# First block's two attentions: probabilities become the stationary operand of the value product, values are streamed, and the division by the softmax sum comes after it

## The chip, the cores and the metric

One core of one Trainium2 chip runs the whole program. The metric is the device time of one execution in microseconds (us), the median of several runs. The core has a matrix engine (TensorE, PE in the profile, its weight loads PEld), a vector engine (DVE), a scalar engine (ACT), a small general engine (POOL) and DMA queues that SyncE (SP) issues. Each engine works through its own queue in order and waits on semaphores of the others.

## What is computed

Two networks follow each other on 512 tokens of width 1024. The change touches only the first one, `first_block`, which has two layers. In each layer one wide projection feeds three branches: a banded attention, a convolution and a dense causal attention. Their outputs are gated, summed and followed by an MLP. The two attentions, cut to what matters:

```python
def swa_attention(q, k, v, sinks, bias, mask):        # 8 query heads, 2 key/value groups, width 64
    scores = einsum('bnqhgd,bnkhd->bnqkhg', qb, kk) * 64 ** -0.5 + bias     # a block of 128 queries,
    scores = where(mask, scores, NEG_INF)                                    # 256 keys: own and last block
    m = maximum(scores.max(axis=3, keepdims=True), sink)
    p = exp(scores - m)
    p = p / (p.sum(axis=3, keepdims=True) + exp(sink - m))
    out = einsum('bnqkhg,bnkhd->bnqhgd', p, vv)

def attend_block(args):                               # mla: 8 heads, blocks of 128 queries, values 64 wide
    sc = (einsum('bqhd,bkhd->bhqk', qn, k_nope) + einsum('bqhd,bkd->bhqk', qp, k_pe)) * scale
    sc = where(key_idx[None, :] <= q_idx[:, None], sc, NEG_INF)
    p = softmax(sc, axis=-1)
    return einsum('bhqk,bkhd->bqhd', p, v)
```

## The kernel before

Activations are kept channel-major: a tile has 128 channels on the partitions and the 512 tokens on the free axis. A projection (`gemm`, `mm3`, L230 to L232) splits each fp32 operand into a high and a low part and adds three products into one PSUM tile `ps_g`, for each of eight chunks of 128 input channels. These products of 128x512 are most of the program. The weights stream in by DMA (`raw`), ACT makes the high part (`whi`, L223) and DVE the low part (`wlo`, L224).

`mix_first` weaves generators: `mla` runs against `inputs` (projections), in layer 0 also against `prep_bias`, and `swa` runs against `branch(2, ...)` (projections again). `weave` fixes the order in which the steps are recorded. The framework then orders each engine's queue by its own plan, so that projection products stand between the steps of an attention. PSUM is split by tag: three banks `g`, two `sc` (scores), and one each of `m`, `tr` (transposes) and `y` (attention output).

`mla` goes over four pairs of heads (`hp`). For each head and each block of 128 queries (`qb`, which sees (qb+1)*128 keys): scores on PE (L740), causal mask, maximum and scaling on DVE, exponential with the row sum on ACT (L771), reciprocal on DVE (L773), a second ACT pass that multiplies the probabilities by it (L774), transposes on PE (L745), and one ACT copy for each 128x128 block into `pT` (L747). After all four query blocks four products follow (L750): the stationary operand is `vt` (128 keys x 64 values), the probabilities stream through (up to 512 queries), and the result lands channel-major in 64 of the 128 rows of `ps_y`, which is then split in high and low part (L203, L204).

`swa` goes over four blocks of queries. For each group `g` of four heads: scores (L796, contraction over 64 rows of `q` and `kk`, the rows of that group), bias added on DVE (L798) into `S`, maximum, exponential (L812), reciprocal, the ACT pass that divides (L818), transposes (L822), a copy to `pT` (L824), and a product with 64 values as stationary operand and 512 columns of probabilities (L825). At the end of a query block `yhi` and `ylo` are cut from `ps_y` (L830, L831).

In PE rows the profile shows an fp32 product as two MATMUL rows with a weight load each, an fp32r product (the projections) or a transpose as one.

Of the kernel before, what the change touches and what calls it, by code (L numbers as in the profile page):

```python
# [20 lines left out]
P = 128  # L21
# [6 lines left out]
class Build:  # L28
# [652 lines left out]
    def mla(self, l, cq, ckv, kpe, out):  # L681
# [28 lines left out]
        for hp in range(4):  # L710
            if hp % 2 == 0:
                ps = self.gemm(W("w_qup", 4 + hp // 2), qs)
                x = self.ch("x", tag="tmp")
                nc.scalar.copy(out=x, in_=ps)
                sw = self.shuffle16(x)
                nc.vector.tensor_tensor(out=x, in0=x, in1=self.cosT, op=ALU.mult)
                nc.vector.tensor_tensor(out=sw, in0=sw, in1=self.sinT, op=ALU.mult)
                qp = self.ch("qp")
                nc.vector.tensor_tensor(out=qp, in0=x, in1=sw, op=ALU.add)
            qh = [self.ch("qh", tag="qh") for _ in range(2)]  # L720
            kh = [self.ch("kh", tag="qh") for _ in range(2)]
# [12 lines left out]
            for i in range(2):  # L734
                h = 2 * hp + i
                pT = [self.ch("pT", tag="pT") for _ in range(4)]
                for qb in range(4):
                    n = (qb + 1) * P
                    ps = self.psum("sc")
                    nc.tensor.matmul(ps[:, :n], qh[i][0:96, qb * P:n], kh[i][0:96, 0:n], start=True, stop=True)  # L740
# [12 lines left out]
            out.append(self.split(yps, tag="y2"))  # L753
# [7 lines left out]
    def softmax_causal(self, ps, n, scale):  # L761

# [11 lines left out]
        nc.scalar.activation(out=pr, in_=pr, func=AF.Copy, scale=r)  # L774
        self.pr = pr

    def swa(self, l, q, kk, v, out):
# [4 lines left out]
        for b in range(4):  # L782
# [3 lines left out]
            yps = self.psum("y")  # L786
            for g in range(2):
                rows = slice(64 * g, 64 * g + 64)
                bias = self.tl([P, 4, 256], F32, "bias")
                nc.sync.dma_start(out=bias, in_=self.biasD[b, 4 * g:4 * g + 4].rearrange("h q k -> q h k"))  # L790
                S = self.tl([P, 4, 256], F32, "S")
                for pr in range(2):
                    ps = self.psum("sc")
                    for i in range(2):
                        c = 2 * pr + i
                        nc.tensor.matmul(ps[:, i * N:(i + 1) * N], q[c][rows, b * P:(b + 1) * P],  # L796
                                         kk[rows, k0:k0 + N], start=True, stop=True)
                    nc.vector.tensor_tensor(out=S[:, 2 * pr:2 * pr + 2, :N],  # L798
                                            in0=ps[:, :2 * N].rearrange("p (i n) -> p i n", i=2),
                                            in1=bias[:, 2 * pr:2 * pr + 2, 256 - N:], op=ALU.add)  # L800
# [3 lines left out]
                sk = sink[:, 4 * g:4 * g + 4]  # L804
                nc.vector.tensor_tensor(out=m, in0=m, in1=sk, op=ALU.max)
                nc.vector.tensor_scalar(out=nm, in0=m, scalar1=-1.0, scalar2=None, op0=ALU.mult)
                es = self.sm("es", 4, "sw4")
                nc.vector.tensor_tensor(out=es, in0=sk, in1=m, op=ALU.subtract)
# [8 lines left out]
                for c in range(4):  # L817
                    nc.scalar.activation(out=S[:, c, :N], in_=S[:, c, :N], func=AF.Copy, scale=r[:, c:c + 1])  # L818
                for kb in range(nk):
# [5 lines left out]
                    nc.tensor.matmul(yps[rows], v[:, b - nk + 1 + kb, rows], pT, start=kb == 0, stop=kb == nk - 1)  # L825
                if g == 0:
                    yield
            sl = slice(b * P, (b + 1) * P)
            for c in range(4):
                nc.scalar.copy(out=yhi[c][:, sl], in_=yps[:, c * P:(c + 1) * P])  # L830
                nc.vector.tensor_tensor(out=ylo[c][:, sl], in0=yps[:, c * P:(c + 1) * P],  # L831
                                        in1=yhi[c][:, sl].bitcast(F32), op=ALU.subtract)
            self.dump_ps(f"ya{l}_{b}", yps)
# [1678 lines left out]
```

## Time and profile before

| | |
|---|---|
| three runs | 3928.62, 3931.33, 3933.89 us; median 3931.33 |
| profiled execution | 3927.74 us, span 3925.7 us (2.0 us lie around the span) |
| PE busy, of the span | 3777.0 us (96%) |
| PEld, DVE, ACT busy | 76%, 61%, 44% |
| mean granted TensorE clock | 0.969 of full speed |
| dense attention, layers 0 and 1 | about 65 to 252 us and 960 to 1085 us of the span |
| banded attention, layers 0 and 1 | about 252 to 330 us and 1085 to 1200 us |

The profile is one execution seen from inside. Busy time says how long an engine had something in flight; idle time before an instruction is put down to what released it. The granted clock has two levels, 1.2 and 2.4 GHz, so 0.5 or 1 in a short stretch and a mean in a longer one.

### The profile page before, as it was taken

The page shows a single profiled execution, that of the slowest core. Times are in us where ns is not written, and L with a number is a line of the kernel's source. Part 1 is how long each engine was busy: PE and PEld are TensorE (multiplying, and loading weights), DVE is VectorE, ACT ScalarE, POOL GpSimd, SP SyncE. Part 2 cuts the span into 40 slices and gives each one's busy share as a digit, 9 for nine tenths or more (in the row PEclk, how much of TensorE's full clock was granted, in tenths as well). Part 3 has the DMA queues.
Part 4 walks back from the last instruction along what each step waited for, and adds up shares of the span by engine and source line. Part 5 has one row for each costly group of instructions (what it writes and reads, how often), then busy time and mean ns, then how long its engine had stood idle before and what let it go on. Part 6 is the DMA issues. An engine that isn't in the chain of part 4 may idle for free.

```text
span 3925.7 us, 54880 instructions
## 1 busy us (share of the span) xinstructions
PE 3777.0 (96%) x21506; PEld 2970.5 (76%) x21506; DVE 2397.6 (61%) x4178; ACT 1741.0 (44%) x3923; POOL 85.0 (2%) x180
## 2 busy tenths in 40 slices
PE   8999999999999999999998999999999999889998
PEld 5566888886667888778885666688888887678887
DVE  7587567665786565657646566454444574756444
ACT  4655343334653333335537788432222264533332
POOL 0000000000000000000001000000000000000000
PEclk9999999999999999999998899899999999889999
DMA  3132345442132355531110000211111212012232
GB/s 129 49 92 83 101 155 180 157 143 65 56 94 85 121 166 171 187 116 45 45 43 2 2 2 2 76 56 64 65 65 65 83 50 68 6 59 95 97 97 75
DMA packets 115699, 324.98 MB, mean 83 GB/s; under 512 B 12528, under 2 KB 34032, under 8 KB 115440
## 3 DMA queue, kind: packets, MB, share of 16 engines
q1 hardware_dynamic: 115440, 321.47, 25.4%
q8 instruction: 169, 2.77, 0.3%
q14 instruction: 90, 0.74, 0.1%
HBM read 307.27 MB, written 12.58 MB: 81 GB/s over the span
## 4 chain that ended last, share of the span: by engine, by line
PE 79%; issue 11%; ACT 5%; DVE 4%; POOL 1%; DMA 0%; POOLq 0%; DVEq 0%; SPq 0%; ACTq 0%
PE ps_g L230 20%; PE ps_g L232 20%; PE ps_g L231 20%; PE ps_mm L1564 1%; PE ps_y L750 1%; ACT B L1621 1%; PE ps_sc L740 1%; PE ps_z L1531 1%; POOL r L308 1%; PE ps_y L825 1%; PE ps_sc L796 1%; PE ps_y L1236 1%; PE ps_lv L1611 1%; PE ps_sc L454 1%; PE ps_lv L1608 1%
## 5 line engine op out<-in xcount | busy, mean ns | idle before, releaser
L230 PE MATMUL ps_g<-hi,whi 128*128 128x512 f32 (+1 forms) x4464 | 1670.5, 374 | 21.2 <-ACT whi L223 13.7
L232 PE MATMUL ps_g<-hi,wlo 128*128 128x512 f32 (+1 forms) x4464 | 1654.9, 371 | 10.5 <-DVE wlo L224 10.4
L231 PE MATMUL ps_g<-lo,whi 128*128 128x512 f32 (+1 forms) x3744 | 1401.4, 374 | 2.3 <-DVE lo L954 1.8
L223 ACT CAST whi<-raw 128x1024 fp32r<-128x1024 f32 (+3 forms) x497 | 481.7, 970 | 1241.8 <-PE ps_g L231 1064.1
L230 PEld LDWEIGHTS ps_g<-hi,whi 128*128 128x128 f32 x4464 | 847.8, 190 | 190.2 <-ACT whi L223 23.8
L232 PEld LDWEIGHTS ps_g<-hi,wlo 128*128 128x128 f32 x4464 | 847.4, 190 | 166.4 <-DVE wlo L224 17.1
L231 PEld LDWEIGHTS ps_g<-lo,whi 128*128 128x128 f32 x3744 | 709.8, 190 | 135.0 <-issue 10.5
L224 DVE TENSOR_TENSOR wlo<-raw,whi 128x1024 fp32r<-128x1024 f32 (+3 forms) x497 | 557.2, 1122 | 165.7 <-ACT whi L223 160.0
L231 PE MATMUL ps_g<-x,whi 128*128 128x512 f32 (+1 forms) x720 | 253.1, 352 | 0.0
L1130 DVE SCALAR_TENSOR_TENSOR x<-ps_g,mod,x 128x512 f32<-128x512 f32 (+1 forms) x192 | 127.0, 662 | 200.3 <-PE ps_g L232 200.1
L879 DVE SCALAR_TENSOR_TENSOR macc<-mraw,cs,macc 128x1024 f32<-128x1024 f32 x140 | 175.7, 1279 | 6.8 <-DMA mraw<-in_mod_w 6.5
L638 DVE SCALAR_TENSOR_TENSOR cv<-u,taps,cv 128x512 f32<-128x512 f32 x240 | 177.1, 744 | 1.1
L1109 DVE TENSOR_SCALAR r<-ps_g 128x512 f32<-128x512 f32 x96 | 57.6, 602 | 180.3 <-PE ps_g L232 180.2
L231 PEld LDWEIGHTS ps_g<-x,whi 128*128 128x128 f32 x720 | 138.5, 192 | 16.5 <-issue 1.6
L589 DVE TENSOR_TENSOR x<-ps_g,x 128x512 f32<-128x512 f32 x64 | 44.2, 690 | 137.8 <-PE ps_g L232 137.8
L473 DVE TENSOR_TENSOR o<-ps_g,R 128x512 f32<-128x512 f32 x76 | 52.2, 689 | 114.6 <-PE ps_g L232 111.7
L1110 ACT ACTIVATE r<-r 128x512 f32<-128x512 f32 x96 | 53.4, 557 | 145.3 <-DVE r L1109 145.3
L308 POOL TENSOR_TENSOR r<-v,mhalf 128x4 f32<-128x4 f32 (+2 forms) x30 | 38.5, 1284 | 2792.5 <-DVE v L327 2135.6
L582 DVE SCALAR_TENSOR_TENSOR r<-ps_g,R 128x512 f32<-128x512 f32 x64 | 44.0, 688 | 80.9 <-PE ps_g L232 77.0
L204 DVE TENSOR_TENSOR lo<-r,hi 128x512 fp32r<-128x512 f32 x96 | 57.6, 600 | 40.7 <-ACT hi L203 40.7
L1621 ACT COPY B<-ps_lv 32x64 f32<-32x64 f32 x384 | 77.5, 202 | 6.4
L291 ACT ACTIVATE sq<-x 128x512 f32<-128x512 f32 (+1 forms) x91 | 49.1, 543 | 70.1 <-DVE x L1130 34.7
(508 smaller groups left out, 4574.3 us busy)
## 6 DMA issues: line engine op xcount, KB each, us to landing
raw<-in_l_mlp_w SPq DMA_DIRECT2D x128, 512.0 KB, 3.5
mraw<-in_mod_w SPq DMA_DIRECT2D x96, 512.0 KB, 4.5
raw<-in_w_in SPq DMA_DIRECT2D x82, 512.0 KB, 3.4
raw<-in_w_up SPq DMA_DIRECT2D x64, 512.0 KB, 3.5
raw<-in_w_down SPq DMA_DIRECT2D x64, 512.0 KB, 3.5
raw<-in_l_w_in SPq DMA_DIRECT2D x50, 512.0 KB, 3.5
raw<-in_w_branch SPq DMA_DIRECT2D x48, 256.0 KB, 2.8
bias<-biasD SPq DMA_DIRECT2D x16, 512.0 KB, 3.9
```

The lines of the kernel that those rows point to most:

```text
L204: nc.vector.tensor_tensor(out=lo, in0=src, in1=hi.bitcast(F32), op=ALU.subtract)
L223: nc.scalar.copy(out=hi, in_=raw)
L224: nc.vector.tensor_tensor(out=lo, in0=raw, in1=hi.bitcast(F32), op=ALU.subtract)
L230: t.matmul(ps, w[0], x[0], start=start, stop=False)
L231: t.matmul(ps, w[0], x[1], start=False, stop=False)
L232: t.matmul(ps, w[1], x[0], start=False, stop=stop)
L308: self.nc.gpsimd.tensor_tensor(out=r, in0=v, in1=self.mhalf[:, :v.shape[1]], op=ALU.pow)
L638: nc.vector.scalar_tensor_tensor(out=y, in0=u[:, j:j + T], scalar=taps[:, c * 31 + j:c * 31 + j + 1], in1=y, op0=ALU.mult, op1=ALU.add)
L879: nc.vector.scalar_tensor_tensor(out=acc[s], in0=rw, scalar=self.cs[:, k, s:s + 1], in1=acc[s], op0=ALU.mult, op1=ALU.add)
L1109: nc.vector.tensor_scalar(out=t, in0=ps[s][:, :n], scalar1=0.0, scalar2=None, op0=ALU.max)
L1130: nc.vector.scalar_tensor_tensor(out=xx[c], in0=ps[:, :n], scalar=md[:, s, 5, c:c + 1], in1=xx[c], op0=ALU.mult, op1=ALU.add)
L1621: nc.scalar.copy(out=B[rows, :, j, :], in_=blocks(ps[rows, 0:64]))
```

## The change

In `mla` the loop over the two heads moves inside the loop over query blocks. The exponentials are transposed as they are, one ACT copy brings all (qb+1) blocks of them to `pT`, and qb+1 products have a 128x128 block of `pT` as stationary operand and 64 columns of `vt` as the streamed one. The result is token-major, 128 queries x 64 values, in the single bank `m`; ACT scales it by the reciprocal on the way to `yq` (L754), and when both heads have written their 64 columns PE transposes `yq` into `ps_y` (L756). The second ACT pass over the probabilities is gone.

In `swa` the outer loop goes over two halves `pr` instead of the groups: each has two heads of group 0 and two of group 1. The four score products alternate between the groups, into two `sc` banks. The bias comes in two DMAs of half the size. The ACT pass over the probabilities is gone; 128x128 blocks of `pT` are stationary and 64 values stream (L835); one DVE multiplication by the reciprocals makes `yq` (L841), and two transposes (L844) bring it to `ps_m`, from which `yhi` and `ylo` are cut.

```diff
@@ mla
-            for i in range(2):
-                h = 2 * hp + i
-                pT = [self.ch("pT", tag="pT") for _ in range(4)]
-                for qb in range(4):
-                    n = (qb + 1) * P
+            for qb in range(4):
+                n = (qb + 1) * P
+                blk = slice(qb * P, n)
+                yq = self.ch("yq", n=P, tag="tmp")
+                for i in range(2):
+                    h = 2 * hp + i
                     ps = self.psum("sc")
...
-                    self.softmax_causal(ps, n, rq[:, qb:qb + 1])
-                    pr = self.pr
+                    pr, r = self.softmax_causal(ps, n, rq[:, qb:qb + 1])
                     tp = self.psum("tr")
                     for kb in range(qb + 1):
                         nc.tensor.transpose(tp[:, kb * P:(kb + 1) * P], pr[:, kb * P:(kb + 1) * P], self.ident)
+                    pT = self.ch("pT", tag="pT")
+                    nc.scalar.copy(out=pT[:, :n], in_=tp[:, :n])
+                    cols = slice(64 * i, 64 * i + 64)
+                    ym = self.psum("m")
                     for kb in range(qb + 1):
-                        nc.scalar.copy(out=pT[kb][:, qb * P:n], in_=tp[:, kb * P:(kb + 1) * P])
+                        nc.tensor.matmul(ym[:, :64], pT[:, kb * P:(kb + 1) * P], vt[kb][:, h * 64:(h + 1) * 64],
+                                         start=kb == 0, stop=kb == qb)
+                    nc.scalar.activation(out=yq[:, cols], in_=ym[:, :64], func=AF.Copy, scale=r)
                     yield
-                for kb in range(4):
-                    nc.tensor.matmul(yps[64 * i:64 * i + 64, kb * P:], vt[kb][:, h * 64:(h + 1) * 64],
-                                     pT[kb][:, kb * P:], start=kb == 0, stop=kb == 3)
+                nc.tensor.transpose(yps[:, blk], yq, self.ident)
@@ softmax_causal
-        nc.scalar.activation(out=pr, in_=pr, func=AF.Copy, scale=r)
-        self.pr = pr
+        return pr, r
@@ swa
-            for g in range(2):
-                rows = slice(64 * g, 64 * g + 64)
+            for pr in range(2):
...
+                ps = [self.psum("sc") for _ in range(2)]
+                for i in range(2):
+                    for g in range(2):
+                        rows = slice(64 * g, 64 * g + 64)
+                        nc.tensor.matmul(ps[g][:, i * N:(i + 1) * N], q[2 * pr + i][rows, b * P:(b + 1) * P],
                                          kk[rows, k0:k0 + N], start=True, stop=True)
...
-                for c in range(4):
-                    nc.scalar.activation(out=S[:, c, :N], in_=S[:, c, :N], func=AF.Copy, scale=r[:, c:c + 1])
...
-                    nc.tensor.matmul(yps[rows], v[:, b - nk + 1 + kb, rows], pT, start=kb == 0, stop=kb == nk - 1)
+                    for c in range(4):
+                        g, h = c // 2, 2 * pr + c % 2
+                        nc.tensor.matmul(yps[:, h * P + 64 * g:h * P + 64 * g + 64], pT[:, c * P:(c + 1) * P],
+                                         v[:, b - nk + 1 + kb, 64 * g:64 * g + 64],
+                                         start=kb == 0 and c == 0, stop=kb == nk - 1, skip_group_check=True)
+                nc.vector.tensor_tensor(out=hv(yq), in0=hv(yps[:, 2 * pr * P:(2 * pr + 2) * P]),
+                                        in1=gi(r).unsqueeze(3).to_broadcast([P, 2, 2, 64]), op=ALU.mult)
+                for i in range(2):
+                    nc.tensor.transpose(yT[:, (2 * pr + i) * P:(2 * pr + i + 1) * P], yq[:, i * P:(i + 1) * P],
+                                        self.ident)
```

The order on the engines is planned anew. PE in the dense attention of layer 1, end of the first head of a pair, before (`ps_g` are projections, `pr` probabilities, operands stand as streamed, stationary):

```order
L745 MATMUL ps_tr_7635<-ident,pr_7628 128x128 x4
L232 MATMUL ps_g_7694<-hi_7059,wlo_7690 128x512
L230 MATMUL ps_g_7694<-hi_7102,whi_7689 128x512
L750 MATMUL ps_y_7490<-pT_7491,vt_7369 64x512
L750 MATMUL ps_y_7490<-pT_7492,vt_7370 64x384
L750 MATMUL ps_y_7490<-pT_7493,vt_7371 64x256
L750 MATMUL ps_y_7490<-pT_7494,vt_7372 64x128
L745 MATMUL ps_tr_7666<-ident,pr_7659 128x128
```

The same engine and layer now, last query block of the first head of a pair:

```order
L746 MATMUL ps_tr_7868<-ident,pr_7862 128x128 x4
L232 MATMUL ps_g_7975<-hi_6968,wlo_7971 128x512
L230 MATMUL ps_g_7975<-hi_7009,whi_7970 128x512
L231 MATMUL ps_g_7975<-lo_7010,whi_7970 128x512
L752 MATMUL ps_m_7875<-vt_7487,pT_7873 128x64
L752 MATMUL ps_m_7875<-vt_7488,pT_7873 128x64
L752 MATMUL ps_m_7875<-vt_7489,pT_7873 128x64
L752 MATMUL ps_m_7875<-vt_7490,pT_7873 128x64
L232 MATMUL ps_g_7975<-hi_7009,wlo_7971 128x512
L230 MATMUL ps_g_7975<-hi_7052,whi_7970 128x512
```

A value product now follows every set of transposes, 64 times in all instead of 16, with a few projection products between the transposes and it. ACT at the same place now (`ps_m` is the bank that each of these products needs):

```order
L748 COPY pT_7873<-ps_tr_7868 128x512
L727 COPY qh_7913<-qp_7571 32x512
L732 COPY kh_7914<-k_1652_7483 32x512
L754 ACTIVATE yq_7856<-ps_m_7875,rec_7866 128x64
L777 ACTIVATE pr_7886,sum_7887<-ps_sc_7881,m_7884,rq_7435 128x512
L732 COPY kh_7915<-k_1652_7483 32x512
```

The scaling that empties `ps_m` stands in ACT's queue behind two copies for the next pair of heads. PE at one set of scores of the banded attention, layer 0, before:

```order
L796 MATMUL ps_sc_2492<-o_2163,q_1587 128x256
L796 MATMUL ps_sc_2492<-o_2163,q_1705 128x256
L796 MATMUL ps_sc_2496<-o_2163,q_1825 128x256
L796 MATMUL ps_sc_2496<-o_2163,q_2000 128x256
L230 MATMUL ps_g_2546<-hi_107,whi_2541 128x512
```

And now, first where the four stand together, then where transposes stand between them:

```order
L804 MATMUL ps_sc_2871<-o_2220,q_1876 128x256
L804 MATMUL ps_sc_2872<-o_2220,q_1876 128x256
L804 MATMUL ps_sc_2871<-o_2220,q_2052 128x256
L804 MATMUL ps_sc_2872<-o_2220,q_2052 128x256
L230 MATMUL ps_g_2939<-hi_107,whi_2934 128x512
```

```order
L804 MATMUL ps_sc_2662<-o_2220,q_1876 128x256
L830 MATMUL ps_tr_2591<-ident,S_2566 128x128
L804 MATMUL ps_sc_2663<-o_2220,q_1876 128x256
L830 MATMUL ps_tr_2591<-ident,S_2566 128x128
L804 MATMUL ps_sc_2662<-o_2220,q_2052 128x256
L830 MATMUL ps_tr_2591<-ident,S_2566 128x128
L804 MATMUL ps_sc_2663<-o_2220,q_2052 128x256
```

The 16 sets were 16 unbroken runs on PE; now they are 28 runs. The 64 value products of `mla` stood in 30 runs and the 28 of `swa` in 28; their successors are products of the full array. From the projections behind the banded attention of layer 1 on, the order on PE, DVE and ACT is what it was.

## Rows read from the trace of the kernel before

**Rows 1.** The page, busy time, share of the span and instructions of TensorE.

```profile
PE 3777.0 (96%) x21506; PEld 2970.5 (76%) x21506; DVE 2397.6 (61%) x4178; ACT 1741.0 (44%) x3923; POOL 85.0 (2%) x180
```

**Rows 2.** Stretch, length, PE, PEld, DVE, ACT, POOL busy (count), clock, DMA, GB/s.

```profile
65.00:252.00 187.00, 183.33 (x798) 102.74 (x796) 122.80 (x265) 112.11 (x266) 0.00 (x0) 0.98 0.20 58
252.00:330.00 78.00, 77.60 (x326) 52.31 (x324) 69.19 (x132) 41.92 (x114) 0.00 (x0) 1.00 0.33 101
960.00:1085.00 125.00, 118.91 (x487) 79.29 (x486) 93.66 (x215) 76.70 (x203) 0.00 (x0) 0.96 0.18 59
```

**Rows 3.** Timeline of PE at L825: start, time in flight, instruction, count.

```profile
263.82 0.40 PE L231 MATMUL ps_g<-lo,whi 128*128 128x512 f32 x1
264.15 1.07 PE L825 MATMUL ps_y<-pT,tok 128*64 128x512 f32 x2
265.15 0.50 PE L232 MATMUL ps_g<-hi,wlo 128*128 128x512 f32 x1
265.49 0.40 PE L230 MATMUL ps_g<-hi,whi 128*128 128x512 f32 x1
265.73 0.40 PE L231 MATMUL ps_g<-lo,whi 128*128 128x512 f32 x1
```

**Rows 4.** Timeline of PE at a broken run of L750.

```profile
250.27 0.50 PE L230 MATMUL ps_g<-hi,whi 128*128 128x512 f32 x1
250.71 0.43 PE L750 MATMUL ps_y<-pT,vt 128*64 128x128 f32 x2
251.07 0.50 PE L231 MATMUL ps_g<-lo,whi 128*128 128x512 f32 x1
251.41 0.39 PE L232 MATMUL ps_g<-hi,wlo 128*128 128x512 f32 x1
```

**Rows 5.** Chain of waits, both attentions: start, time on the chain, instructions.

```profile
141.30 2.30 PE ps_y L750 x8
253.18 1.09 PE ps_sc L796 x8
268.43 1.92 PE ps_sc L796 x8
```

**Rows 6.** Timeline of PE at fp32 products of 128x128 stationary, 64 streamed columns.

```profile
2027.94 1.45 PE L1291 MATMUL ps_mm<-cv,t 128*128 128x64 f32 x12
2029.19 0.48 PE L230 MATMUL ps_g<-hi,whi 128*128 128x512 f32 x1
2029.51 0.40 PE L231 MATMUL ps_g<-x,whi 128*128 128x512 f32 x1
```

**Rows 7.** Timeline of PE at single transposes between projection products.

```profile
1097.60 0.48 PE L231 MATMUL ps_g<-lo,whi 128*128 128x512 f32 x1
1097.92 0.27 PE L822 MATMUL ps_tr<-ident,S 128*128 128x128 f32 x1
1097.95 0.48 PE L232 MATMUL ps_g<-hi,wlo 128*128 128x512 f32 x1
```

**Rows 8.** Timeline of PE: 64-row products of both halves of the rows.

```profile
3424.49 1.71 PE L2159 MATMUL ps_g<-qd,kd 64*128 64x128 f32 x16
```

**Rows 9.** Timeline of PE, layer 1, from one pair of heads to the next.

```profile
1006.33 0.66 PE L745 MATMUL ps_tr<-ident,pr 128*128 128x128 f32 x4 [1.50 <-ACT pr L774]
1007.85 3.88 PE L750 MATMUL ps_y<-pT,vt 128*64 128x512 f32 x8 [0.87 <-ACT pT L747]
1013.05 0.92 PE L740 MATMUL ps_sc<-kh,qh 96*128 96x128 f32 x4 [1.31 <-ACT kh L732]
```

**Rows 10.** Busy time by stretch: around the rows before.

```profile
1003.00:1022.00 19.00, 14.65 (x44) 8.97 (x43) 9.80 (x26) 12.84 (x31) 0.00 (x0) 0.73 0.29 96
```

**Rows 11.** ACT: L774 by line (min/median/max ns), two copies by form (busy, mean).

```profile
L774 ACT ACTIVATE pr<-pr,rec x64: 393/557/752, 73.1 to 1079.2; 128x128 f32<-128x128 f32 x16, 128x256 f32<-128x256 f32 x16, 128x384 f32<-128x384 f32 x16, 128x512 f32<-128x512 f32 x16
L824 ACT COPY pT<-ps_tr 128x512 f32<-128x512 f32 x28 | 16.4, 587 | 27.8 <-PE ps_tr L822 27.5
L1679 ACT COPY zs<-ps_z 128x64 f32<-128x64 f32 x96 | 20.0, 210 | 20.3 <-PE ps_z L1676 18.5
```

More of the change, by code (lines that the diff above doesn't have):

```diff
@@ L733, in mla @@
             yps = self.psum("y")
-            for i in range(2):
-                h = 2 * hp + i
-                pT = [self.ch("pT", tag="pT") for _ in range(4)]
-                for qb in range(4):
-                    n = (qb + 1) * P
+            for qb in range(4):
[4 more added lines that the diff above has]
+                    h = 2 * hp + i
                     ps = self.psum("sc")
-                    nc.tensor.matmul(ps[:, :n], qh[i][0:96, qb * P:n], kh[i][0:96, 0:n], start=True, stop=True)
-                    self.softmax_causal(ps, n, rq[:, qb:qb + 1])
-                    pr = self.pr
+                    nc.tensor.matmul(ps[:, :n], qh[i][0:96, blk], kh[i][0:96, 0:n], start=True, stop=True)
+                    pr, r = self.softmax_causal(ps, n, rq[:, qb:qb + 1])
                     tp = self.psum("tr")
@@ L785, in swa @@
             k0 = 0 if b == 0 else (b - 1) * P
-            yps = self.psum("y")
-            for g in range(2):
-                rows = slice(64 * g, 64 * g + 64)
+            yps, yT = self.psum("y"), self.psum("m")
+            for pr in range(2):
                 bias = self.tl([P, 4, 256], F32, "bias")
-                nc.sync.dma_start(out=bias, in_=self.biasD[b, 4 * g:4 * g + 4].rearrange("h q k -> q h k"))
+                for g in range(2):
+                    h = 4 * g + 2 * pr
+                    nc.sync.dma_start(out=bias[:, 2 * g:2 * g + 2],
+                                      in_=self.biasD[b, h:h + 2].rearrange("h q k -> q h k"))
                 S = self.tl([P, 4, 256], F32, "S")
[L792 to L796, printed above, removed]
+                ps = [self.psum("sc") for _ in range(2)]
+                for i in range(2):
+                    for g in range(2):
+                        rows = slice(64 * g, 64 * g + 64)
+                        nc.tensor.matmul(ps[g][:, i * N:(i + 1) * N], q[2 * pr + i][rows, b * P:(b + 1) * P],
                                          kk[rows, k0:k0 + N], start=True, stop=True)
-                    nc.vector.tensor_tensor(out=S[:, 2 * pr:2 * pr + 2, :N],
-                                            in0=ps[:, :2 * N].rearrange("p (i n) -> p i n", i=2),
-                                            in1=bias[:, 2 * pr:2 * pr + 2, 256 - N:], op=ALU.add)
+                for g in range(2):
+                    nc.vector.tensor_tensor(out=S[:, 2 * g:2 * g + 2, :N],
+                                            in0=ps[g][:, :2 * N].rearrange("p (i n) -> p i n", i=2),
+                                            in1=bias[:, 2 * g:2 * g + 2, 256 - N:], op=ALU.add)
                 m = self.sm("m", 4, "sw4")
@@ L803, in swa @@
                 nm = self.sm("nm", 4, "sw4")
-                sk = sink[:, 4 * g:4 * g + 4]
-                nc.vector.tensor_tensor(out=m, in0=m, in1=sk, op=ALU.max)
+                gi = lambda t: t.rearrange("p (g i) -> p g i", i=2)
+                sk = sink.rearrange("p (g h) -> p g h", g=2)[:, :, 2 * pr:2 * pr + 2]
+                nc.vector.tensor_tensor(out=gi(m), in0=gi(m), in1=sk, op=ALU.max)
                 nc.vector.tensor_scalar(out=nm, in0=m, scalar1=-1.0, scalar2=None, op0=ALU.mult)
                 es = self.sm("es", 4, "sw4")
-                nc.vector.tensor_tensor(out=es, in0=sk, in1=m, op=ALU.subtract)
+                nc.vector.tensor_tensor(out=gi(es), in0=sk, in1=gi(m), op=ALU.subtract)
                 nc.scalar.activation(out=es, in_=es, func=AF.Exp)
@@ L824, in swa @@
                     nc.scalar.copy(out=pT, in_=tp)
[L825 to L826 removed]
+                    for c in range(4):
[3 more added lines that the diff above has]
+                                         start=kb == 0 and c == 0, stop=kb == nk - 1, skip_group_check=True)
+                yq = self.ch("yq", n=256, tag="tmp")
+                hv = lambda t: t.rearrange("p (i g f) -> p g i f", g=2, f=64)
+                nc.vector.tensor_tensor(out=hv(yq), in0=hv(yps[:, 2 * pr * P:(2 * pr + 2) * P]),
[3 more added lines that the diff above has]
+                                        self.ident)
+                if pr == 0:
                     yield
@@ L829, in swa @@
             for c in range(4):
-                nc.scalar.copy(out=yhi[c][:, sl], in_=yps[:, c * P:(c + 1) * P])
-                nc.vector.tensor_tensor(out=ylo[c][:, sl], in0=yps[:, c * P:(c + 1) * P],
+                nc.scalar.copy(out=yhi[c][:, sl], in_=yT[:, c * P:(c + 1) * P])
+                nc.vector.tensor_tensor(out=ylo[c][:, sl], in0=yT[:, c * P:(c + 1) * P],
                                         in1=yhi[c][:, sl].bitcast(F32), op=ALU.subtract)
-            self.dump_ps(f"ya{l}_{b}", yps)
+            self.dump_ps(f"ya{l}_{b}", yT)
             yield
```

## The prediction, on record before the run

> **What bounds the kernel now.** I read busy time first: PE has something in flight for 96% of the span [rows 1]. Then the stretches with the attentions. The dense attentions last 187 and 125 us, with PE busy for 183.3 and 118.9, so PE idles 3.7 and 6.1 us there; in layer 0's banded attention it idles 0.4 of 78 us [rows 2]. PE is the bound in all of them, and projection products fill whatever time the attention leaves. So the change is worth what PE's own queue gets shorter, plus what PE's few waits lose or gain. Third, the timeline of PE, for starts from one instruction to the next: the time in flight of a row overlaps its neighbours, only starts tell what an instruction costs the queue. A projection product takes 0.23 to 0.24 us that way (265.49 to 265.73, [rows 3]).
>
> **Value products of the banded attention.** One product of 512 columns with 64 values as stationary operand stands between projections that start at 263.82 and 265.49 [rows 3]. That is 1.67 us, less two spacings of 0.23: 1.21 us. About 0.1 us of it lies ahead of its start (0.33 instead of 0.23) and 0.11 behind (265.15 to 265.49, again instead of 0.23): PE pauses when it goes from a product that uses all 128 columns of the array to one that uses 64, and back. 28 of them are 33.9 us. They are replaced by 112 products with a 128x128 stationary block and 64 streamed columns, two passes each. The trace has the same form elsewhere: twelve passes start at 2027.94, and the second projection behind them at 2029.51 [rows 6]; 1.57 less 0.23 is 1.34, or 0.112 a pass. 224 passes are 25.1 us. Gain 8.8 us.
>
> **Value products of the dense attention.** An unbroken set for one head takes 2.30 us on the chain [rows 5], with the 0.1 ahead and 0.1 behind 2.5; 16 heads are 40 us. They stand in 30 runs, so 14 sets are broken once more. What a break costs, a short run shows: projections at 250.27 and 251.41 with two passes of 128 columns between [rows 4], 1.14 less 0.46 is 0.68, of which two passes of 128 columns explain 0.2 (2560 column passes in 2.30 us). So 0.45 for a run by itself, 6 us for 14. Together 46 us, against 160 products or 320 passes of 0.112, 35.8 us. Gain 10 us.
>
> A rule of the Trainium skill speaks against both of these. "TensorEngine Tiling (Array Packing)", section Performance Considerations, recommends for 64 wide right-hand sides to swap stationary and streamed operand and to pack two column tiles, which is the form that is given up here; packed, the old 2.30 us would be 1.15 for a head, 18 us for all, and the change would cost some 17 us on this term. The trace does not bear it out: the eight passes of a head all use one half of the columns and follow each other over 2.30 us, so nothing was packed that could be lost.
>
> **Transposes added.** 32 in each attention. One between two projections costs 1097.95 less 1097.60 less 0.23, 0.12 us [rows 7]. 64 are 7.7 us. Loss.
>
> **Scores of the banded attention.** Eight passes of 256 columns are 1.92 us on the chain, of 128 columns 1.09 [rows 5]. The difference says 0.83 us for eight times 128 columns; what is left of the 1.09, 0.26, and the 0.2 around a run as above make 0.47 us for each run. The 16 sets were 16 runs and are 28 in the new order: 12 more runs, 5.6 us lost. Against that the two groups use different halves of the array's rows, and alternate. Do such products run side by side? L2159 has eight passes of 128 columns on one half and then eight on the other. Its sixteen are in flight for 1.71 us [rows 8]; one after the other they would need 0.26 and 1.66, and 0.27 until the last one lands (the flight of a transpose, [rows 7]), 2.2. Half a us is gained at the seam alone, so I take overlap as real. Of the 16 sets six alternate without a break, five in part and five not at all (pairs of one group, or single products between transposes). A full one saves 0.83 us, 0.42 in the first query block; in all 6 to 7 us. Scores thus cost 0 with overlap, 5.6 us without.
>
> **Sum on PE's queue**: 8.8 + 10 - 7.7 - 0 = 11 us less; without overlap 5.5.
>
> **Waits.** ACT loses 64 passes of 0.557 us (median of L774, [rows 11]), 36 us in the dense attention, and 64 more passes in the banded one. It gains 64 scalings of 128x64, 0.21 each by the nearest row [rows 11], 13 us. That matters where PE waits for ACT, above all at the change of head pairs in layer 1: waits of 1.50 for L774, 0.87 for L747 and 1.31 for L732 [rows 9], and behind them TensorE is granted 0.73 of its clock over 19 us [rows 10], at which 5.1 us are lost. I count half of these 3.7 and 5.1 us as won, 4.4 us: the pass of 0.73 us at this place goes, the copies and casts stay. Against it stand new hops. A value product now follows each of 64 sets of transposes instead of 16. From the start of the last transpose it takes 0.27 us until it lands [rows 7] and 0.59 for the longest copy [rows 11], 0.86; the order puts three projections (0.69) and the transpose's own 0.12 there, 0.81. So 0.05 us short where nothing else is in ACT's queue, 3 us in all. The bounds: nothing, if shorter copies leave slack, and 10 us, if one hop in four meets a copy of 0.59 us ahead of it on ACT. Net 1 us won; bounds 9 us won, 10 lost.
>
> **Counted at nothing.** The 16 multiplications of `yq` on DVE: at most 0.59 us each (an ACT copy of twice the columns), 4.7 us in a layer, beside 69.2 busy of 78 [rows 2]; they fit, barely, and convolution steps move later. Without that cover they cost up to 4.7 us a layer. The 16 more DMA issues for the bias move the same bytes; the next `S` needs them only after the transposes of the last one, and PE idles 0.4 us in that stretch, so there is slack now; a late bias would stall one set of scores.
>
> All of it against the profiled execution, 3927.7 us: 12 us less is 3915.7. The median of the runs shown is 3.6 us higher, and so is the forecast: 3931.3 - 12 = 3919 us.
>
> **The rivals.** (1) *Nothing measurable.* The scores do not overlap, or the many short runs eat it, which leaves 5.5 us; and the new hops cost what the lighter ACT gives. 3926 us, between 3924 and 3939, as its bounds on the hops fall. For it: the 28 runs, and how little cover 0.81 us against 0.86 is. Against it: rows 8.
> (2) *All waits at the change of pairs vanish*, with them the lost clock: 11 and 9 us, 3911 us. For it: the three waits of layer 1 hang on one queue, ACT, which gets lighter just there. Against it: two of them are for copies that stay.
> (3) *Slower: one bank for every hop.* `ps_m` is one bank. Each of the 64 value products must wait until ACT's scaling L754 has emptied it for the one before, and that scaling stands in ACT's queue behind copies (two of about 0.59 us in the order shown); in layer 0 `prep_bias` uses the same bank 32 times for L442. These are 96 hand-overs. With 0.2 us lost at each the 12 us are used up and 8 more, 3939 us; that is the point from which it is slower. For it: ACT is busy 112 of 187 us in layer 0's dense attention [rows 2], so something often stands ahead, and a late value product holds up every projection behind it on PE. Against it: at the place shown nine projections, 2 us, stand before the next product into that bank, against 1.2 us of copies and 0.2 of scaling.
>
> **How the numbers follow.** Forecast (8 to 15 us less): 0.47. Rival 1: 0.29. Rival 2: 0.13. Rival 3: 0.11. A measurement of this kernel can tell about 0.2%, 8 us, from no change. Faster is the forecast and rival 2, 0.60; within 0.2% rival 1, 0.29; slower rival 3, 0.11. The range leaves out rival 3, a part of rival 1's upper end and the best of rival 2: 3907 to 3932 us. The forecast's own range is 3916 to 3923.
>
> **What the next profile would show.** L835 and L752 at 0.11 us from pass to pass, and projections next to them without the 0.1 us pause; a set of L804 with 256 columns at about 1.1 us where it alternates, 1.9 where it doesn't. Idle PE of 3.7 and 6.1 us in the dense attentions should not grow by more than 3 us, and the stretch with a clock of 0.73 should shrink. Wrong would be: L752 and L835 passes that take longer, since a new block of weights comes with every 64 columns (at 0.13 us 10 us more); or waits of PE for L754 through `ps_m`, rival 3; or alternating scores that follow each other, rival 1.

## The result, and the profile after

| | before | after |
|---|---|---|
| median of the timed runs | 3930.62 us (3928.62 to 3933.89, 4 runs) | 3967.23 us (3959.26 to 3979.52, 4 runs) |
| ratio, 95% interval | | 1.0101 (1.008 to 1.0121) |
| profiled execution | 3927.74 us | 3979.52 us, span 3977.7 |

The change makes the kernel 37 us slower, 1.0%. The forecast was 3919 us with a range to 3932: wrong in sign.

The page's first part of after, against [rows 1]:

```profile
PE 3811.2 (96%) x21930; PEld 3031.4 (76%) x21930; DVE 2407.8 (61%) x4194; ACT 1698.8 (43%) x3763; POOL 85.8 (2%) x180
```

ACT got 42 us lighter, and the share of PE is the same 96%: this view shows no cause. The place does show when one follows the projection products (L230 to L232). Both kernels have 13704 of them in nearly the same sequence, so the time between two of them, counted from their starts in the trace, compares stage with stage, whatever moved around them. "150 to 600" is the time from the product that has 150 others ahead of it to the one that has 600:

| us, profiled executions | before | after | difference |
|---|---|---|---|
| 150 to 600: layer 0, dense attention, bias table, start of the banded one | 216.9 | 264.7 | +47.8 |
| 600 to 900: layer 0, banded attention and what follows | 103.1 | 102.0 | -1.1 |
| 3200 to 3400: layer 1, first half of the dense attention | 85.0 | 77.6 | -7.4 |
| 3400 to 3600: its second half | 75.2 | 78.1 | +2.9 |
| 3600 to 3900: layer 1, banded attention | 107.6 | 104.6 | -3.0 |

Layer 1 gained 7.5 us. Layer 0 lost 46.7, all of it ahead of product 600. (The profiled execution is the slowest of the four, 12 us above the median; behind product 3900, where nothing is changed, it takes 15 us more than the one before.) All stage times, here and below, are those of one profiled execution of each kernel. The busy times by stretch of after, first the stage 150 to 600 in two parts, then the worst piece of it, then layer 1's two stages, columns as in [rows 2]:

```profile
62.00:178.00 116.00, 105.58 (x484) 63.44 (x484) 63.94 (x132) 53.73 (x113) 0.00 (x0) 0.90 0.18 55
178.00:327.00 149.00, 137.79 (x605) 89.30 (x603) 88.16 (x188) 63.31 (x150) 0.00 (x0) 0.85 0.20 58
240.00:302.00 62.00, 53.22 (x204) 32.91 (x203) 21.32 (x58) 24.87 (x62) 0.00 (x0) 0.67 0.13 38
940.00:1131.00 191.00, 180.53 (x873) 135.36 (x872) 131.44 (x286) 94.44 (x206) 5.41 (x3) 0.96 0.17 54
1131.00:1236.00 105.00, 103.64 (x546) 79.36 (x545) 93.55 (x184) 46.92 (x129) 0.00 (x0) 1.00 0.32 96
```

From 62 to 327 us PE idles 116.00 - 105.58 + 149.00 - 137.79 = 21.6 us, against 3.7 in the same stage before. And the granted clock is 0.90 and 0.85 there: 0.10 of 116 and 0.15 of 149, 34 us, against some 4 before. 18 us more of waiting and 30 us more lost at half clock make up the 48 us, nearly: some 3 of the 30 fall on time in which PE idles anyway. Between 240 and 302 us the clock is 0.67, and DVE and ACT together have 46 us of work in 62: no engine is full, the stage is a chain.

What PE waited for in this stage and up to 400 us (engine, what waited, what for, us in total, times, longest), without the groups that concern neither the attention, the bias table nor DVE's part of the weights:

```profile
PE ps_tr L746 <- ACT pr L777: 9.2, 6, 2.4
PE ps_sc L454 <- DVE oh L451: 3.2, 5, 0.9
PE ps_g L232 <- DVE wlo L224: 3.0, 1, 3.0
PE ps_m L442 <- ACT yq L754: 2.4, 6, 0.4
PE ps_m L752 <- ACT pT L748: 2.1, 2, 1.5
...
PE ps_sc L454 <- ACT oh L449: 1.3, 2, 1.0
...
PE ps_m L752 <- ACT dd L448: 0.8, 1, 0.8
```

Two of them are hand-overs of bank `m`: the bias products L442 wait for the dense attention's scaling L754, and the value products L752 for `prep_bias`'s L448. They are small, 3.2 us. The larger ones are ordinary steps of the two generators with nothing left to cover them, as the chain of waits shows (start, time on the chain):

```profile
266.05 1.39 PE ps_sc L454 x3
267.44 1.06 PE ps_m L752 x4
268.50 0.02 issue
268.52 0.32 ACT yq L754
268.85 0.04 issue
268.89 0.64 PE ps_m L442 x4
269.53 0.03 issue
269.56 0.76 DVE oh L451
270.32 0.04 issue
270.36 1.44 PE ps_sc L454 x3
271.80 0.83 PE ps_tr L746 x3
272.63 1.28 PE ps_sc L742 x2
273.91 0.74 PE ps_m L752 x6
```

Read it from the bank: a value product fills `m`, ACT empties it (L754), a bias product fills it (L442), DVE or ACT empties it (L451, L448), and so on, one after the other, with no projection product in between. PE's order says why there is none: 525 projection products stand ahead of the first scores of layer 0's banded attention, and the last product of `prep_bias` (L454) and the last dense scores stand behind all of them. In the kernel before they stand behind 461 and 483, with 516 ahead of the banded scores. The starts of the projections show what it costs: between the 525th and the one after it 40.6 us pass (249.2 to 289.7 us), and before, the longest such gap between products 150 and 600 is 7.9 us. The order could be counted before the run; the experiments show that the count alone doesn't give the price.

### The profile page after: what moved, and what is told of

Read it like the earlier page. It is cut to its first block, busy times and chain, and to the rows that moved or that the text cites. A ratio compares the mean times of both kernels' runs of the same rounds, so it can differ in the third digit from the quotient of the medians.

```text
span 3977.7 us, 55738 instructions
## 1 busy us (share of the span) xinstructions
PE 3811.2 (96%) x21930; PEld 3031.4 (76%) x21930; DVE 2407.8 (61%) x4194; ACT 1698.8 (43%) x3763; POOL 85.8 (2%) x180
## 4 chain that ended last, share of the span: by engine, by line
PE 78%; issue 11%; ACT 5%; DVE 4%; POOL 1%; DMA 0%; POOLq 0%; DVEq 0%; SPq 0%; ACTq 0%
PE ps_g L230 20%; PE ps_g L232 20%; PE ps_g L231 19%; PE ps_mm L1584 1%; PE ps_m L752 1%; PE ps_sc L742 1%; PE ps_z L1551 1%; POOL r L308 1%; ACT B L1641 1%; PE ps_lv L1631 1%; PE ps_sc L454 1%; PE ps_y L1256 1%; PE ps_y L835 1%; PE ps_lv L1628 1%; ACT whi L223 1%
## 5 line engine op out<-in xcount | busy, mean ns | idle before, releaser
L230 PE MATMUL ps_g<-hi,whi 128*128 128x512 f32 (+1 forms) x4464 | 1673.4, 375 | 21.4 <-ACT whi L223 12.1
L232 PE MATMUL ps_g<-hi,wlo 128*128 128x512 f32 (+1 forms) x4464 | 1658.4, 372 | 12.4 <-DVE wlo L224 12.2
L230 PEld LDWEIGHTS ps_g<-hi,whi 128*128 128x128 f32 x4464 | 849.2, 190 | 178.5 <-ACT whi L223 20.6
L232 PEld LDWEIGHTS ps_g<-hi,wlo 128*128 128x128 f32 x4464 | 848.3, 190 | 158.3 <-DVE wlo L224 19.2
L473 DVE TENSOR_TENSOR o<-ps_g,R 128x512 f32<-128x512 f32 x76 | 52.1, 688 | 102.5 <-PE ps_g L232 99.1
L204 DVE TENSOR_TENSOR lo<-r,hi 128x512 fp32r<-128x512 f32 x96 | 57.7, 602 | 40.7 <-ACT hi L203 40.7
```

The lines of the kernel that those rows point to most:

```text
L204: nc.vector.tensor_tensor(out=lo, in0=src, in1=hi.bitcast(F32), op=ALU.subtract)
L230: t.matmul(ps, w[0], x[0], start=start, stop=False)
L232: t.matmul(ps, w[1], x[0], start=False, stop=stop)
```

## The experiments

Theory 1: bank `m`, shared in layer 0 by value products and `prep_bias`, makes both generators late; when the projections run out, their steps lie bare and the clock falls. In form 1a each hand-over costs, wherever it stands; in form 1b it costs only where the two generators outlive the projections that cover them. Theory 2: the dense attention's own longer chain of hops does it. Theory 3: it is the banded attention. The kernel before ran again beside each group of experiments: its median was 3931.35 us beside the kernels with one attention changed and the two that take the sharing away, 3931.34 beside those with 60 bias steps and the one with bank `tr`, and 3927.54 beside the last four (from `IN_STEPS` 12 on). Each ratio is to that; it can differ from the quotient of the medians by 0.1%.

**Which attention.** The dense one alone (with the softmax), and the banded one alone, each taken from the changed kernel.

```diff
@@ first kernel: swa
-            for pr in range(2):
+            for g in range(2):
...
@@ second kernel: mla, softmax_causal
-            for qb in range(4):
+            for i in range(2):
...
```

> The dense attention and the softmax as changed, the banded attention as before. Theories 1 and 2: the loss is all in the dense attention of layer 0, so it stays; the banded attention's terms of the prediction (8.8 us on value products, less 3.9 for its 32 transposes, scores 0) are missing: 3972 us. Theory 3: 3920 us.

Measured: 3970.15 us, ratio 1.0099 (1.0078 to 1.0119).

> The banded attention as changed, the dense attention and the softmax as before. Theories 1 and 2: 3926 us (3931 less 8.8 plus 3.9, scores 0), or 3932 if alternating score products gain nothing (5.6 us more). Theory 3: 3965 us or more.

Measured: 3938.38 us, ratio 1.0018 (1.0005 to 1.0032). The dense attention alone has the whole loss by the medians, 39 us; 150 to 900 takes 356.5 us against 319.9. Theory 3 falls. The banded attention did not gain 5 us but lost some 7 in the medians; by stages it lost 2.2 us in layer 0 and won 0.5 in layer 1. Two things take its gain in this trace: in layer 0 L232 waits 2.0 us for `wlo` on DVE; and the clock, of which below. The other 5 us of the medians stand in no stage of the attentions (behind product 3900, where nothing is changed, this execution takes 4.5 us more); their cause is not shown.

**The bank.** First the kernel before, with nothing changed but the bank of the bias products, so that they share one with the transposes (the order on PE is planned anew with it):

```diff
@@ prep_bias
-                ps = self.psum("m")
+                ps = self.psum("tr")
```

> The kernel before, but the bias products of `prep_bias` (L442 there) write into the single bank `tr`, which the dense attention's transposes use 32 times in layer 0; `m` stays empty there. Nothing of the change is in it, only a bank that the two generators hand to each other. In the order on PE all 525 projections stand before the last bias product and the last scores, as in the changed kernel. Theories 1a and 1b: it loses as the changed kernel did in layer 0, 3965 to 3980 us. Theory 2: 3928 to 3938 us, since the dense attention's own chain is the old one.

Measured: 3964.15 us, ratio 1.0091 (1.0073 to 1.0109). 150 to 900 takes 356.0 us, 36 more than before, and the stretch of the stage 150 to 600 shows the same two losses (23 us idle, clock 0.94):

```profile
63.00:310.00 247.00, 223.95 (x932) 128.43 (x931) 150.66 (x314) 124.77 (x305) 0.00 (x0) 0.94 0.19 58
```

The gap behind the 525th projection is 28.5 us here. So a shared bank alone does to the old kernel nearly what the change did to it: the median lies 1 us below theory 1's range and 26 above theory 2's, which fails as the main cause. Next the changed kernel with the sharing taken away, in two ways: the bias products into a bank `g`, or the value products into the columns of `ps_y` that are filled only later.

```diff
@@ prep_bias (first kernel)
-                ps = self.psum("m")
+                ps = self.psum("g")
@@ mla (second kernel)
-                    ym = self.psum("m")
+                    ym = yps[:, qb * P + 64 * i:qb * P + 64 * i + 64]
...
```

> The changed kernel, but the four broadcast products of `prep_bias` (L442) write into one of the three `g` banks instead of bank `m`; everything else as changed. Theory 1 (in layer 0 the value products L752 and the bias products L442 hand one bank `m` to each other, 32 times each, so both generators end late, the projections are used up before them, and TensorE idles at half clock between about 240 and 302 us): the 45 us lost there come back and the gains of layer 1 stay, 3915 to 3928 us; in the order on PE 480 projections stand before the last scores of layer 0 instead of all 525. Theory 2 (the longer chain of hops inside the dense attention itself ends late, whoever shares the bank): 3955 to 3970 us. Theory 3 (the loss is the banded attention's): 3955 to 3970 us.

Measured: 3940.69 us, ratio 1.0027 (1.0009 to 1.0046), between the ranges of theory 1 and the others.

> The changed kernel, but the value products of the dense attention (L752) write into the columns of `ps_y` that the transpose of `yq` fills later, so bank `m` is left to `prep_bias` as before. Theory 1 in its plain form: 3915 to 3928 us as well. But in the order on PE all 525 projections still stand before the last bias product and the last scores of layer 0, as in the changed kernel; if what counts is that the projections run out, and the hand-over has only moved to bank `y`, 3940 to 3965 us. Theory 2: 3955 to 3970 us. Theory 3: 3955 to 3970 us.

Measured: 3927.18 us, ratio 0.999 (0.9975 to 1.0005). With `ps_y` layer 0 takes 326.0 us from 150 to 900 instead of 366.7: sharing costs 40.7 us of the 46.8, and the medians differ by 40. What the order on PE suggested (all 525 products ahead of the end, so 3940 us or more) did not come true: behind the 525th projection 11.6 us pass instead of 40.6. An end without cover is short when the generators don't hand one bank to each other. Bank `g` gives back less, 335.3 us, because the projections want that bank: there L230 waits 4.3 us for L448, the ACT step that empties it.

**When.** The changed kernel, the kernel before, and the kernel with `ps_y`, with the bias table recorded earlier:

```diff
-IN_STEPS, BIAS_STEPS, CTX_STEPS = 13.7, 39.7, 12
+IN_STEPS, BIAS_STEPS, CTX_STEPS = 13.7, 60, 12
```

> The changed kernel with one number of the weave changed: BIAS_STEPS 60 instead of 39.7, so that `prep_bias` is recorded ahead of the dense attention's steps and ends earlier. Bank `m` is still shared, with as many hand-overs. In the order on PE 468 projections of layer 0 stand before the last scores and 399 before the last bias product, instead of all 525. Theory 1a (each hand-over of the shared bank costs, wherever it stands): 3950 to 3967 us. Theory 1b (the shared bank makes both generators late, and it costs only where they outlive the projections that cover their waits): 3920 to 3932 us. Theory 2 (the dense attention's own chain of hops is too long, whoever shares the bank): 3940 to 3965 us.

Measured: 3950.6 us, ratio 1.0045 (1.0029 to 1.0061).

> The kernel before with the same number, BIAS_STEPS 60: the control for the run above. No theory has a reason for a change beyond what a measurement can tell: 3925 to 3937 us.

Measured: 3933.61 us, ratio 1.0007 (0.9995 to 1.0019).

> The changed kernel with both: value products of the dense attention in `ps_y`, BIAS_STEPS 60. Theory 1b: no tail and no sharing, layer 0 no worse than before, 7 us of gain in layer 1 left: 3918 to 3927 us. Theory 1a: the same, since nothing is shared. Theory 2: 3940 us or more.

Measured: 3935.07 us, ratio 1.0009 (0.9995 to 1.0024), between the ranges. With the bank shared, half of the loss is gone: 3950.6 us is far from theory 1b's range, at the lower edge of 1a's and within theory 2's. The end is nearly covered now (products 350 to 600 take 104.2 us, in the control 99.1), but the early part pays: products 150 to 350 take 140.0 us with 17 of them idle, against 119.4 and 4.4 in the control, and the projections have gaps of 31.0 and 24.2 us there, where the control's longest is 6.3. Moving a chained pair of generators moves the bare stretch; it doesn't remove it. Part of that is not bank `m`: with `ps_y` the same products still take 133.5 us, at a mean clock of 0.87, with gaps of 18.5 and 19.7 us. That execution, 3950.46 us, is the slowest of its twelve, so its stage is longer than usual; and the two generators still share the two banks `sc`, as in the kernel before. No run here took that away.

A last try on what `ps_y` leaves in layer 0, 6 us, was to keep projections back (`IN_STEPS if l else 12`):

> The changed kernel with the value products of the dense attention in `ps_y`, and in layer 0 the weave's IN_STEPS 12 instead of 13.7, which keeps projections back: 500 of 525 stand before the last scores. The kernel with `ps_y` alone lost 6 us in layer 0 still. Theory 1b (what is left there is the end without projections): they come back, 3918 to 3925 us. Theory 2 (what is left is the dense attention's own chain of hops): 3925 to 3935 us.

Measured: 3925.45 us, ratio 1.0006 (0.9993 to 1.0019); 150 to 900 takes 327.0 us. Theory 1b is wrong for this rest: with products left over at the end it stays in the trace. The new form of both attentions costs 6 to 7 us in layer 0; what they consist of stands at the end of the next section.

**The gain without the loss.** Layer 0 as before, layer 1 as changed; then the banded attention of layer 0 changed too; then, in the first of them (called e11 in an expectation below), the score loops exchanged.

```diff
@@ mix_first (mla0 and swa0 are mla and swa of before)
-        main = [(self.mla(l, cq, ckv, kpe, yc), 36), (inputs(), IN_STEPS)]
+        main = [((self.mla if l else self.mla0)(l, cq, ckv, kpe, yc), 36), (inputs(), IN_STEPS)]
...
-        self.weave([(self.swa(l, q, kv[0], kv[1], ya), 8),
+        self.weave([((self.swa if l else self.swa0)(l, q, kv[0], kv[1], ya), 8),
...
@@ swa (third kernel only)
-                for i in range(2):
-                    for g in range(2):
+                for g in range(2):
+                    for i in range(2):
```

> Layer 0 with both attentions as before, layer 1 with both as changed, so nothing shares bank `m` with `prep_bias`. Theory 1 (the loss is the shared bank's, in layer 0): layer 0 takes as long as before, and the 7.4 us that the changed kernel gained between the projections 3200 and 3900 (layer 1) stay, 3920 to 3929 us. Theory 4 (the terms of the sum were wrong too, and layer 1's gain was only the clock of one execution): 3929 to 3937 us.

Measured: 3923.23 us, ratio 0.999 (0.998 to 1.0). From 150 to 900 it takes 319.1 us, as before; from 3200 to 3900 260.3, as in the changed kernel, against 267.8. The median lies where theory 1 put it; but 4 us are less than a measurement can tell for sure. Theory 4 falls only in part: other kernels with both old attentions in layer 1 take 263.2 (the control with 60 bias steps) and 264.6 us (bank `tr`) from 3200 to 3900, so the gain is 3 to 7.5 us, and the upper part of it is the clock of the one execution before.

> The run above with the changed banded attention in layer 0 too; the dense attention of layer 0 stays as before. By the prediction's sum for the banded attention 2.5 us less than the run above. By what the kernel with the banded attention alone showed in layer 0 (a clock of half for 6.8 us and a wait of 2.0 us of L232 for DVE) about 2 us more.

Measured: 3922.52 us, ratio 0.9989 (0.998 to 0.9999). The wait of 2.0 us of L232 came, the half clock did not, and 0.7 us of difference decides nothing between the two sums. This and the next are the best versions; 0.1% is too little to call them faster.

> The kernel of e11, with the two loops around the score products of layer 1's banded attention exchanged: both products of one group, then both of the other, in the same two banks. The order on PE is otherwise the same. If alternating row halves overlap, as the prediction took: a full set of eight passes of 256 columns takes 1.9 to 2.1 us instead of 1.3, and layer 1 is about 3 us longer. If they follow each other: no difference.

Measured: 3921.98 us, ratio 0.9989 (0.9979 to 0.9998); no difference from the first. By the expectation that would mean that the products follow each other, but the trace says something else. PE's timeline at the same set of eight passes of score products, split by two transposes, in the alternating order of the first kernel:

```profile
1139.81 0.70 PE L954 MATMUL ps_sc<-o,q 64*128 64x256 f32 x4
1140.44 0.44 PE L994 MATMUL ps_m<-ident,yq 128*128 128x128 f32 x2
1140.81 0.70 PE L954 MATMUL ps_sc<-o,q 64*128 64x256 f32 x4
```

and in group order, behind a set that is not split:

```profile
1106.39 1.14 PE L954 MATMUL ps_sc<-o,q 64*128 64x256 f32 x8
...
1140.58 1.13 PE L954 MATMUL ps_sc<-o,q 64*128 64x256 f32 x4
1141.64 0.44 PE L994 MATMUL ps_m<-ident,yq 128*128 128x128 f32 x2
1142.00 1.13 PE L954 MATMUL ps_sc<-o,q 64*128 64x256 f32 x4
```

Four passes of one group take 1.13 us, four of both groups 0.70, and eight that take one group after the other 1.14: not longer than four. The halves of the rows overlap as soon as both groups stand in one run, in whatever order. So the expectation was wrong to take it for granted that group order keeps them apart. Only the split sets lose, 0.85 us each, and there are two in the layer. The Trainium skill agrees ("TensorEngine Tiling (Array Packing)", section Key Properties): products in different tiles of the array can go in parallel.

## Why the prediction was wrong, step by step

**The failed step is the term of the waits, "Net 1 us won": it holds nothing for the bank `m` that two generators share in layer 0.** That stood only in rival 3, at a chance of 0.11 and a price of 0.2 us for each hand-over. What the runs showed in its place: the stage of layer 0 takes 47.8 us more, and 40 us come back when the value products get other columns. Rival 3 named the right bank ("`prep_bias` uses the same bank 32 times"), but it was judged at a place in layer 1, where nothing shares the bank: nine projections before the next product, so enough cover. That held in layer 1, where L752 waits 0.2 us in all and for a copy, not for the bank. In layer 0 the cover is the same set of projections for two generators, and that they run out ahead of both was written in the order.

Its price was wrong too. 96 hand-overs at 0.2 us are 19 us, and PE's idle time in that stage grew by 18; but that is luck. Only 64 of the 96 lie in layer 0, 13 us, and the waits for the bank itself are 3.2 us; the rest of the idle time is at ordinary steps of a chain that lies bare. And the clock was left out, which took 30 us more as PE's work thinned out. How much it takes isn't fixed: with the dense attention alone PE idles as long in that stage (21.5 us), and some 20 us more than before are lost to the clock; with bank `tr` 23 us come with 11 more.

There is a page for the hand-over itself: the Trainium skill ("PSUM — Partial Sum Buffer", section Summary: rules for kernel authors) tells to let matmuls go to another bank than the one being read; with one bank for two generators that becomes a wait, 2.4 us in all of L442 for L754 here.

**Waits in layer 1:** about as said. The sum has 4.4 us won at the change of pairs [rows 9, 10] and half of the 3 lost at hops, 2.9; from product 3200 to 3600 PE idles 6.2 us instead of 8.5. The 2.9 us lost from 3400 to 3600 are mostly such a wait: PE idles 2.8 us there instead of 0.4, 1.6 of them before L742 for L732's copy at 1093 us. Of the 7.5 us that layer 1 gained from 3200 to 3900, 3.4 are the clock (6.8 us lost to it before, 3.4 after), 1.2 idle time, and some 3 are left for PE's queue, for which 5.5 were counted. That 7.5 comes near the 8 that the sum gives for this layer is thus part luck: the clock of the one execution before makes up for terms that were too large.

**Value products, dense, 10 us won:** mis-sized. PE's timeline at runs of eight and of two passes, and at a transpose of `yq`:

```profile
1050.37 0.39 PE L230 MATMUL ps_g<-hi,whi 128*128 128x512 f32 x1
1050.60 1.02 PE L752 MATMUL ps_m<-vt,pT 128*128 128x64 f32 x8
1051.42 0.48 PE L231 MATMUL ps_g<-lo,whi 128*128 128x512 f32 x1
1051.74 0.39 PE L232 MATMUL ps_g<-hi,wlo 128*128 128x512 f32 x1
...
1029.53 0.39 PE L230 MATMUL ps_g<-hi,whi 128*128 128x512 f32 x1
1029.81 0.43 PE L752 MATMUL ps_m<-vt,pT 128*128 128x64 f32 x2
1030.05 0.48 PE L231 MATMUL ps_g<-lo,whi 128*128 128x512 f32 x1
1030.37 0.40 PE L232 MATMUL ps_g<-hi,wlo 128*128 128x512 f32 x1
1030.65 0.33 PE L756 MATMUL ps_y<-ident,yq 128*128 128x128 f32 x1
1030.73 0.48 PE L230 MATMUL ps_g<-hi,whi 128*128 128x512 f32 x1
1031.05 0.39 PE L231 MATMUL ps_g<-lo,whi 128*128 128x512 f32 x1
```

Eight passes cost 1051.74 - 1050.37 - 2 x 0.23 = 0.91 us, 0.114 a pass, as said. Two cost 1030.37 - 1029.53 - 0.46 = 0.38, 0.19 a pass. In the same way runs of four and six, at 999.56 and 1008.85 us, cost 0.48 and 0.82. A head needs one of each, 2.59 us instead of 2.24, so 16 heads 41.4 us instead of 35.8: 4.6 won, not 10.

**Transposes, 7.7 us lost:** the single one of `yq` costs 1031.05 - 1030.37 - 0.46 = 0.22 us, where 0.12 was counted. The trace of before has both prices: single transposes of L822 between projections cost 0.12 or 0.20 us and more. 32 are 7.0 us instead of 3.8; those of the banded attention go in pairs at 0.23 a pair and are as said. So by these prices the dense attention's queue got 2 us longer rather than 6 shorter, about half of it in each layer.

**Banded attention:** its terms were right in size. Eight passes of L835 cost 0.90 us, 0.113 a pass, against 1.21 for the product before. Rival 1 was that the scores don't overlap: they do. A full set of L804 that stands alone between projections costs 1.26 us (their starts at 339.95 and 341.67 us, less 0.46), as forecast. By stages 3.0 us are won in layer 1, where 2.5 were counted; with the old dense attention beside it the same stage takes 107.6 us, as before, 1.7 us of it lost to the clock. **Counted at nothing** was DVE's multiplication, with up to 4.7 us a layer if not covered. The wait of 3.0 us of L232 for `wlo`, among the waits above, is the nearest thing to it: it ends at 396.40 us, and from 385.47 to 395.13 DVE goes through a multiplication of `yq` (0.42 us), the cuts of `ylo` and convolution steps before it comes to that `wlo`. The multiplication is a small part of these 9.7 us. The wait belongs to the banded attention (2.0 us with that alone, 0.2 before); that it is the multiplication and not the new order of DVE's steps is not shown. The halved bias transfers left no wait of PE behind.

**Rival 2** (all waits at the change of pairs vanish, 3911 us) did not come true in layer 1 either: L742 still waits 2.4 us for L732's copies there.

The 6 us that `ps_y` leaves in layer 0 are not a longer queue. From product 150 to 900 PE idles 11.1 us instead of 5.7, and 7 us instead of 3 are lost to the clock; what is left is some 3 us shorter than before, since the banded attention's queue got shorter by more than the dense one's got longer. Most of the idle time is new behind product 600, where L232 waits 3.0 us for `wlo` and L835 1.9 us for L832's copies: the banded attention's part. What stays open: why these waits come, and why an early bias table leaves bare stretches even when bank `m` isn't shared.

## What to carry to other kernels

Before a new use of a single PSUM bank is costed, list who else takes that bank in each stage in which the code runs: two generators that share one become one chain, and the price is not the hand-overs but the cover that both use up. Count in the order of the waiting engine how much covering work still stands behind the last step of each chain; 525 of 525 ahead of it was a warning here. It is a warning and not a price: with `ps_y` the same 525 stood ahead of the last scores, and layer 0 lost 6 us instead of 47. And price idle time of TensorE with its clock, as a range: 18 us more of waiting came with 30 us more here, and about as much waiting with 20 and with 11 in two other kernels.

## What the runs showed of the hardware that was not expected

**The clock fell without a wait.** In the kernel with the banded attention alone PE's timeline has from 275.44 us four single transposes, each ahead of a pair of passes on 64 rows, and then half clock; the last of the four:

```profile
278.04 0.33 PE L825 MATMUL ps_tr<-ident,S 128*128 128x128 f32 x1
278.30 0.70 PE L799 MATMUL ps_sc<-o,q 64*128 64x256 f32 x2
278.93 0.74 PE L230 MATMUL ps_g<-hi,whi 128*128 128x512 f32 x1
279.47 0.63 PE L231 MATMUL ps_g<-lo,whi 128*128 128x512 f32 x1
```

The same in busy times by stretch, PE busy throughout, the granted clock third from the end:

```profile
275.40:278.90 3.50, 3.50 (x13) 1.59 (x11) 3.50 (x7) 2.31 (x6) 0.00 (x0) 1.00 0.30 75
278.90:286.00 7.10, 7.10 (x28) 6.31 (x27) 1.65 (x3) 0.68 (x2) 0.00 (x0) 0.52 0.28 78
```

So 3.4 us were lost at 1.2 GHz with PE in flight all the time. The mixture of short forms would be the nearest reading, but it is not enough. In the kernel with layer 1 changed and the banded attention of layer 0 too, the same four transposes and pairs of passes stand at the same place, from 274.42 to 277.90 us, with the same times; behind them the clock stays:

```profile
274.40:277.90 3.50, 3.50 (x13) 1.59 (x11) 3.50 (x7) 2.29 (x6) 0.00 (x0) 1.00 0.29 75
277.90:285.00 7.10, 7.10 (x43) 6.14 (x43) 4.42 (x9) 1.81 (x4) 0.00 (x0) 1.00 0.45 148
```

One sequence, two outcomes: the 3.4 us belong to one execution, and what decided is open.

**The row halves overlap in any order** within a run (eight passes in 1.14 us, four of one half in 1.13), and a short run of 128x128 blocks with 64 streamed columns costs more a pass, though not evenly: 0.19 us for two, 0.12 for four, 0.137 for six, 0.114 for eight.
